# Two output projections with tokens on the partitions, norms from per-token sums, and the second layer's input transposed by diag(1/rms)

## The chip, the cores and the metric

The kernel runs on one core of one Trainium2 chip. A core has five engines with their own instruction streams: TensorE (PE, with its weight loads shown as PEld), VectorE (DVE), ScalarE (ACT), GpSimd (POOL) and SyncE (SP), which issues the transfers here. Work is held in SBUF, products are summed in PSUM, and inputs and outputs lie in DRAM. The metric is device time in microseconds (us), the median of several runs; lower is better.

## The reference

Two layers act on 256 context tokens and 256 latent tokens of width 2048. Each layer norms its input, scales and shifts it by vectors computed from a conditioning vector, projects it, mixes it in two branches, projects the result back with a 2048x2048 matrix, norms that, multiplies it by a gate vector and adds it to the stream:

```python
for i in range(DEPTH):                       # DEPTH = 2
    need_ctx = i < DEPTH - 1
    sh_x, sc_x, gt_x = jnp.split(cond_x @ ada_w[i] + ada_b[i], 3, axis=-1)
    sh_c, sc_c, gt_c = jnp.split(cond_c @ ada_w[i] + ada_b[i], 3, axis=-1)
    u_x = modulate(rms_norm(h_x, pre_g[i]), sh_x, sc_x)
    u_c = modulate(rms_norm(h_c, pre_g[i]), sh_c, sc_c)
    # i = 0: out = [conv branch | Fourier branch] @ ab_w_out
    # i = 1: out = [neighbourhood attention | S5 state space] @ cd_w_out (latents alone)
    ...
    h_x = h_x + gt_x[:, None] * rms_norm(out_x, post_g[i])
    if need_ctx:
        h_c = h_c + gt_c[:, None] * rms_norm(out_c, post_g[i])
return h_x
```

So between the layers there are two norms in a row for each token: one over the projection `out` (call its factor r1), and one over the new stream h1 = h0 + r1 * gate * post_g * out (factor r2). The second layer's input is u = h1 * r2 * A + shift, with A and the shift per feature.

## The kernel before

All arithmetic is float32. A product is built from exact halves: weights and inputs are split into a high and a low part (`split`, L70 to L76: ACT writes the high part `wh`, DVE or POOL the low part `wl`), and each product takes three matmuls (high x high, high x low, low x high). Weights stream through `load_w` (L299) as chunks of two row tiles of 512 columns, 512 KB each, loaded by SP into `raw`; eight chunks make one column group of 512 output columns over 2048 rows. `next_w` keeps three chunks ahead. `group` (its matmuls are L460) runs one column group over "blocks". A block is one accumulator, either feature-major (`mov`: a 128-column piece of the weights is stationary, the tokens move past it, and the output has features on the partitions) or token-major (`sta`: 128 tokens are stationary and the weights move past). `step` is called after each chunk: `step_ada` there does a piece of the second layer's conditioning product (`E`, L143), whose chunks SP loads as `raw<-in_ada_dram`.

The order within each engine comes from a scheduler that emits instructions by priority (`tc.high_priority()` lets a piece go earlier); only the POOL of the stretch between the layers is written out by hand (`pool_order`).

The layer-0 output projection works feature-major. Column groups n4 = 0, 1, 2 run all 512 tokens at once, with accumulators `acc`. The last one, n4 = 3, runs in two halves, hf = 0 for the context tokens and hf = 1 for the latents, with 256 columns in each matmul and accumulators `ao`. `out0_evac` empties each accumulator: ACT squares it, ACT multiplies it by the gate column (once for each half, `oG`), ACT squares that, DVE multiplies it by the residual input (`h0r`), and DVE adds the three products into running sums `aS`. `mid_chain(hf)` then turns these sums into both factors: PE sums over the partitions by a matmul with ones (`pc`, L865), DVE does two reciprocal square roots in steps on 128x2 tiles (L85 to L91) and the algebra between them, DVE writes a diagonal (`dg`, L105), PE spreads it over all partitions (`pr`, L112) and ACT copies it to SBUF (`R`, L114). With R, POOL forms h1 feature by feature (`oG*R`, L904, and `+h0s`, L905), and DVE and ACT build the input of layer 1 from it (`build_u`: DVE `w`, L183; ACT `uh`, L184; DVE `ul`, L185).

Layer 1 begins with the keys and values of the first head pair (`kv`), context tokens first and latents next, so that the first half can run while the second is normed. Then comes the S5 projection (`acc` again, token-major), and then the attention with its projections (`aq`, `ag` and others).

The layer-1 output projection is feature-major as well: 768 matmuls of 256 columns (`ao` again), ACT squares and gates each accumulator, DVE adds the squares (`sacc`). After the last matmul come the sums over partitions (`pc`), one reciprocal square root, the diagonal, its spread (`pr`), `R`, and then 32 DVE and POOL instructions on 128x256 tiles (L1419 times the factor, L1421 plus the residual) with eight output transfers of 256 KB.

Of the kernel before, what the change touches and what calls it, by code (L numbers as in the profile page):

```python
# [40 lines left out]
def tile_backbone(ctx: ExitStack, tc: tile.TileContext, a):  # L41
# [52 lines left out]
    def col_sums(psp, acc, n=4, tag="ps"):  # L94
        """acc [features, n*128 tokens] -> PSUM [tokens, n, 2] sums over the features."""
# [5 lines left out]
    def spread(psp, r, n, out, tag="ps"):  # L101
        """r [tokens, n] -> out [all partitions, n*128 tokens]."""
# [21 lines left out]
    def ada_finish(psp, l, q, es, tag="ps"):  # L124
        """es: [4 x 32 rows, 512] partial products -> columns of ada[l]."""
# [20 lines left out]
    # A = (1 + scale) * pre_g ; ada columns of chunk q < 8: [sc 2q, sc 2q+1, sh 2q, sh 2q+1]  # L146
# [14 lines left out]
    Gt = [cp.tile([P, KT, 2], F32, name="Gt%d" % l) for l in range(2)]  # L161

    def gate_cols(l):
# [15 lines left out]
    def build_u(l, kt, h, R, halves):  # L179
        """u = h * R * A + shift, split; h [P, 512] and R (per token) for the halves given."""  # L180
# [9 lines left out]
    def mm3(ps, wh, wl, xh, xl, start, stop):  # L190
        """ps += w.T @ x from the exact halves."""
# [23 lines left out]
    ss0 = cp.tile([P, 4], F32, name="ss0")  # L215
# [72 lines left out]
    wpool = ctx.enter_context(tc.tile_pool(name="wpool", reuse_waits="tile", bufs=1))  # L288
    # the chunks in the order of their use
# [22 lines left out]
    def next_w():  # L312
        """The next pair of row tiles; the loads and splits run ahead."""
# [25 lines left out]
    WAIT = 99.0  # the next part comes with the next chunk  # L339
# [23 lines left out]
    def ada_vec(l, qs, nm, pool, eng):  # L363
        """The same on VectorE or GpSimd (and ScalarE), for the first nm columns."""
# [1180 lines left out]
```

## Time and profile before

| | |
|---|---|
| median of 3 runs | 1590.17 us (1589.27 to 1592.42) |
| span of the profiled execution | 1588.4 us |
| median less span | 1.8 us |
| PE busy | 1481.1 us (93%) |
| DVE busy | 1085.7 us (68%) |
| ACT busy | 604.8 us (38%) |
| POOL busy | 306.9 us (19%) |

The profile gives the span of one execution and no time of its own beside it; the 1.8 us between the span and the median are taken as what lies around the span. In the profile's page the span is cut into 40 slices of 39.7 us. PE's busy share is nine tenths or more in nearly all of them. Exceptions are the first slice, five slices near the middle (eight, eight, nine, nine and eight tenths), which hold the stretch between the layers, and the last slice, with the end of the kernel. The granted clock of TensorE (PEclk) is full but for two slices in that same stretch and the last one. A busy PE is thus the rule, and the places where it isn't are the ones in which the order of the other engines shows.

### The profile page before, as it was taken

How to read it: one execution, taken by the hardware profiler on the slowest of the kernel's cores; microseconds unless marked ns; L12 is line 12 of the kernel's file. 1: busy time of each engine (PE TensorE's matmuls, PEld its weight loads, DVE VectorE, ACT ScalarE, POOL GpSimd, SP SyncE). 2: the span in 40 equal slices, each digit the busy share in tenths (PEclk: the TensorE clock that was granted, in tenths of full speed). 3: DMA queues.
4: the chain of work that ended last, by engine and by line, in shares of the span. 5: the costliest groups of instructions: out<-in, count | busy, mean ns of one | idle time of the engine just before them, and what ended most of it. 6: DMA issues, size and time to landing. Idle time of an engine off the chain costs nothing.

```text
span 1588.4 us, 23466 instructions
## 1 busy us (share of the span) xinstructions
PE 1481.1 (93%) x8786; PEld 1213.1 (76%) x8786; DVE 1085.7 (68%) x2460; ACT 604.8 (38%) x1155; POOL 306.9 (19%) x301
## 2 busy tenths in 40 slices
PE   3999999999999999999968899889999999999995
PEld 1556767777877657787957798777888979899995
DVE  5244999999665555674898937769597785636555
ACT  4232112121224132432533436564464554425542
POOL 0000000010020000000264605684243343000001
PEclk9999999999999999999988999999999999999997
DMA  9875444444244566653548536552232322425552
GB/s 387 346 309 211 159 159 159 159 172 166 86 159 153 185 226 210 215 191 133 176 138 280 159 117 210 168 184 101 90 124 84 110 100 98 142 83 183 187 198 80
DMA packets 80179, 269.94 MB, mean 170 GB/s; under 512 B 8513, under 2 KB 20289, under 8 KB 75329
## 3 DMA queue, kind: packets, MB, share of 16 engines
q1 hardware_dynamic: 80064, 268.44, 48.0%
q8 instruction: 69, 1.13, 0.3%
q14 instruction: 46, 0.37, 0.1%
HBM read 264.21 MB, written 4.19 MB: 169 GB/s over the span
## 4 chain that ended last, share of the span: by engine, by line
PE 69%; DVE 17%; DMA 5%; ACT 4%; issue 3%; POOL 2%; SPq 0%; DVEq 0%; ACTq 0%; POOLq 0%
PE acc L460 31%; PE kv L460 9%; PE ao L460 8%; PE E L143 4%; DVE wl L76 4%; DMA raw<-in_ada_dram 3%; PE aq L460 2%; PE ag L460 2%; PE acc L193 2%; PE acc L194 2%; PE adg L460 1%; ACT wh L73 1%; DVE w L183 1%; PE acc L192 1%; PE po L1290 1%
## 5 line engine op out<-in xcount | busy, mean ns | idle before, releaser
L73 ACT ACTIVATE wh<-raw 128x1024 fp32r<-128x1024 f32 (+1 forms) x264 | 273.3, 1039 | 574.2 <-PE acc L460 246.3
L76 DVE TENSOR_TENSOR wl<-raw,wh 128x1024 fp32r<-128x1024 f32 (+1 forms) x259 | 325.5, 1261 | 213.8 <-ACT wh L73 209.6
L495 DVE SCALAR_TENSOR_TENSOR cv<-ain,cw,cv 128x512 f32<-128x512 f32 x240 | 170.4, 749 | 0.0
L460 PE MATMUL acc<-uh,wh 128*128 128x512 f32 x400 | 160.5, 401 | 2.2 <-ACT wh L73 1.7
L460 PE MATMUL acc<-uh,wl 128*128 128x512 f32 x400 | 156.9, 397 | 2.2 <-DVE wl L76 2.2
L460 PE MATMUL acc<-ul,wh 128*128 128x512 f32 x400 | 157.4, 393 | 0.0
L460 PE MATMUL kv<-wh,uh 128*128 128x256 f32 x384 | 110.6, 288 | 3.2 <-DVE sg L1335 3.2
L460 PE MATMUL kv<-wl,uh 128*128 128x256 f32 x384 | 109.9, 286 | 0.0
L460 PE MATMUL kv<-wh,ul 128*128 128x256 f32 x384 | 109.6, 285 | 0.0
L460 PEld LDWEIGHTS acc<-uh,wh 128*128 128x128 f32 x400 | 75.4, 188 | 40.2 <-issue 10.9
L378 DVE SCALAR_TENSOR_TENSOR pa<-raw,condS,pa 128x512 f32<-128x512 f32 x90 | 63.3, 746 | 55.9 <-DMA raw<-in_ada_dram 50.1
L460 PE MATMUL kv<-ul,wh 128*128 128x512 f32 (+1 forms) x224 | 83.6, 377 | 18.2 <-DVE ul L185 18.1
L460 PEld LDWEIGHTS acc<-uh,wl 128*128 128x128 f32 x400 | 75.8, 189 | 21.1 <-DVE wl L76 2.8
L460 PE MATMUL kv<-uh,wh 128*128 128x512 f32 (+1 forms) x224 | 84.5, 391 | 3.9 <-ACT uh L184 3.9
L460 PEld LDWEIGHTS acc<-ul,wh 128*128 128x128 f32 x400 | 75.5, 189 | 16.1 <-issue 0.8
L460 PE MATMUL kv<-uh,wl 128*128 128x512 f32 (+1 forms) x224 | 82.7, 373 | 0.0
L384 POOL TENSOR_TENSOR pa<-pa,raw 128x512 f32<-128x512 f32 x45 | 64.8, 1441 | 79.1 <-ACT raw L383 77.7
L460 PEld LDWEIGHTS kv<-wh,uh 128*128 128x128 f32 x384 | 75.2, 196 | 5.8 <-DVE sg L1335 4.1
L76 POOL TENSOR_TENSOR wl<-raw,wh 128x1024 fp32r<-128x1024 f32 x5 | 12.0, 2429 | 335.5 <-DVE aS L852 333.1
L460 PEld LDWEIGHTS kv<-wl,uh 128*128 128x128 f32 x384 | 75.3, 196 | 1.8
L460 PE MATMUL acc<-wl,uh 128*128 128x512 f32 x192 | 76.5, 398 | 0.0
L460 PE MATMUL acc<-wh,ul 128*128 128x512 f32 x192 | 76.4, 398 | 0.0
(403 smaller groups left out, 3819.0 us busy)
## 6 DMA issues: line engine op xcount, KB each, us to landing
raw<-in_w_dram SPq DMA_DIRECT2D x184, 512.0 KB, 3.6
raw<-in_ada_dram SPq DMA_DIRECT2D x128, 512.0 KB, 4.8
raw<-in_wo_dram SPq DMA_DIRECT2D x72, 512.0 KB, 4.1
aw<-in_ada_dram SPq DMA_DIRECT2D x32, 1024.0 KB, 6.8
w<-in_w0a_dram SPq DMA_DIRECT2D x8, 896.0 KB, 6.8
h<-in_h_dram SPq DMA_DIRECT2D x4, 1024.0 KB, 8.3
h0r<-in_h_dram SPq DMA_DIRECT2D x16, 256.0 KB, 3.4
h0s<-in_h_dram SPq DMA_DIRECT2D x16, 256.0 KB, 4.6
```

The source lines that it names most:

```text
L73: S.activation(hi, src, AF.Copy)
L76: slo.tensor_tensor(lo, src, hi.bitcast(F32), ALU.subtract)
L143: T.matmul(E[32 * g:32 * g + 32, :], condS[:, kt, :], raw, start=(kt < 4), stop=(kt >= 12), skip_group_check=True)
L183: V.scalar_tensor_tensor(w, h[:, c], Am[l][:, kt, m:m + 1], rr, ALU.mult, ALU.mult)
L192: T.matmul(ps, wh, xh, start=start, stop=False)
L193: T.matmul(ps, wh, xl, start=False, stop=False)
L194: T.matmul(ps, wl, xh, start=False, stop=stop)
L378: V.scalar_tensor_tensor(acc, wj, c, acc, ALU.mult, ALU.add)
L384: eng.tensor_tensor(acc, acc, pr, ALU.add)
L460: T.matmul(out, lt, rt, start=st and m == 0, stop=en and m == 2, skip_group_check=True)
L495: ins = V.scalar_tensor_tensor(o, x[:, :, k:k + L], cw05[:, ch, k:k + 1], o, ALU.mult, ALU.add)
L1290: T.matmul(po, vT[:, k, i * P:(i + 1) * P], U_["PT"][:, k, :], start=k == 0, stop=k == 3)
```

## The change

Both output projections are turned token-major. An accumulator then has 128 tokens on its partitions and 512 features along the row, so a sum over features is a sum along the row: ACT's Square writes it as a by-product (`accum_out`), and no matmul with ones and no spread is needed. What was a column (the gate per feature) becomes a row that is the same on all partitions; what was a row (the factor per token) becomes a column. Layer 1 still wants features on the partitions, so h1 goes through PE once more.

- `gate_cols` becomes `gate_rows`: the gate vector is transposed on PE, copied by ACT, written to DRAM and loaded back spread over 128 partitions as 128x512 tiles (eight for layer 0, four for layer 1).
- `out0_evac` is one ACT Square with its row sum and one DVE multiply from PSUM by the gate tile. The 32 sums, 256-column evacuations and `h0r` products go.
- The last column group of layer 0 runs two blocks of 512 columns for each half: 96 matmuls of 512 columns each instead of 192 of 256.
- `mid_chain` reduces the sums, takes the root, forms h1 on DVE (8 instructions on 128x512, `oG*r1 + h0t`), squares it on ACT (8), takes the second root and writes ident * r2 for two token tiles (`dg`, 128x128 each).
- `u1_pair`: four PE matmuls on 128x128 tiles (`z`) give h1 * r2 transposed; then ACT `w<-z` with the scale A, ACT `uh`, DVE `ul`. DVE's `w` and POOL's two steps go.
- `h0t` (the residual input, token-major) is loaded once, 16 tiles of 256 KB, instead of `h0r` and `h0s`, 16 of 256 KB each.
- The conditioning product's last part for now (8 chunks, 16 `E` matmuls) falls into the last column group of layer 0 instead of the first `kv` groups.
- At the end, each token tile has its own root and four DVE instructions on 128x512 with four output transfers; the last column group runs its last three chunks block by block.

```diff
-    def out0_evac(f, ps, c):
...
-        S.activation(sq, ps, AF.Square)
-        for m, h in ((1, CT), (0, XT)):
-            if c.start <= h.start < c.stop:
-                o = h.start - c.start
-                S.activation(oG[f][:, h], ps[:, o:o + L], AF.Copy, scale=Gt[0][:, f, m:m + 1])
-        S.activation(s3, oG[f][:, c], AF.Square)
-        pr = h0r[f][:, c]
-        V.tensor_tensor(pr, oG[f][:, c], pr, ALU.mult)
-        for acc, t in zip(aS, (sq, pr, s3)):
...
+    def out0_evac(t, n4, ps):
...
+        jk = scr.tile([P, 512], F32, tag="t512", name="jk")
+        S.activation(jk, ps, AF.Square, accum_out=ssq[:, 0, t, n4:n4 + 1])
+        V.tensor_tensor(oG[t][n4], ps, gts[n4, 1 - t // 2], ALU.mult)
...
     def mid_chain(hf):
...
+            r1 = token_rsqrt(ssq[:, 0, ts, :], 2, "r1_%d" % hf, "r2")
+            for i in range(2):
+                t = 2 * hf + i
+                for c in range(4):
+                    o = oG[t][c]
+                    V.scalar_tensor_tensor(o, o, r1[:, i:i + 1], h0t[t, c], ALU.mult, ALU.add)
+                    jk = scr.tile([P, 512], F32, tag="t512", name="jk")
+                    S.activation(jk, o, AF.Square, accum_out=ssq[:, 1, t, c:c + 1])
+            r2 = token_rsqrt(ssq[:, 1, ts, :], 2, "r2_%d" % hf, "r2")
+            dg = l0.tile([P, 2, P], F32, tag="pa%d" % hf, name="dg")
+            for i in range(2):
+                V.tensor_scalar(dg[:, i, :], ident, r2[:, i:i + 1], None, ALU.mult)
...
+    def u1_pair(hf, p, pool, tag):
...
+                T.matmul(z[:, j, i * P:(i + 1) * P],
+                         oG[2 * hf + i][kt // 4][:, (kt % 4) * P:(kt % 4 + 1) * P],
+                         dgs[hf][:, i, :], start=True, stop=True)
...
+            S.activation(w, z[:, j, :], AF.Copy, scale=Am[1][:, kt, m:m + 1])
+            S.activation(uh[kt][:, c], w, AF.Identity, bias=sh_col(1, kt, m))
+            V.scalar_tensor_tensor(ul[kt][:, c], w, sh_col(1, kt, m), uh[kt][:, c].bitcast(F32),
+                                   ALU.add, ALU.subtract)
...
+    for hf in range(2):
+        group(KORD0, [blk(accs[t], 0, 512, sta=lambda k, t=t: mtok(k, t))
+                      for t in (2 * hf, 2 * hf + 1)], tail=2, step=step_pairs)
+        for t in (2 * hf, 2 * hf + 1):
+            out0_evac(t, 3, accs[t])
+        mid_chain(hf)
```

DVE at the end of the first half's chain, before. `rr` holds the factors, `dg` is the diagonal that PE's spread waits for, and `w` is the first step of layer 1's input.

```order
L89 TENSOR_TENSOR r2t<-rr 128x2
L90 TENSOR_TENSOR r2t<-r2t,r2n 128x2
L91 SCALAR_TENSOR_TENSOR rr<-r2t,rr 128x2
L105 TENSOR_TENSOR dg<-ident,rr 128x512
L76 TENSOR_TENSOR wl<-raw,wh 128x1024 x2
L183 SCALAR_TENSOR_TENSOR w<-oG_4933,Am_81,R_0_6137 128x256
L852 TENSOR_TENSOR aS_4376<-aS_4376,ev 128x256
```

DVE at the same place after: the context tokens' second chain (`r_0`, ending in `dg`), with the last accumulator of the latents (`ao_5551`), the latents' sums and a weight split between its steps.

```order
L91 SCALAR_TENSOR_TENSOR r_0_5786<-r2t,r_0_5786 128x2
L853 TENSOR_REDUCE sm<-ssq 128x2
L848 TENSOR_TENSOR oG_5540<-ao_5551,gt 128x512
L89 TENSOR_TENSOR r2t<-r_0_5786 128x2
L855 TENSOR_SCALAR ms<-sm 128x2
L90 TENSOR_TENSOR r2t<-r2t,r2n 128x2
L76 TENSOR_TENSOR wl<-raw,wh 128x1024
L87 TENSOR_SCALAR r2n<-ms 128x2
L91 SCALAR_TENSOR_TENSOR r_0_5786<-r2t,r_0_5786 128x2
L85 TENSOR_SCALAR r2t<-ms 128x2
L875 TENSOR_SCALAR dg<-ident,r_0_5786 128x128 x2
```

The context tokens' diagonal stands behind the multiply of the last accumulator, where before it stood some 20 instructions ahead of the latents' evacuation.

ACT at the beginning of layer 1, before: the latents' last evacuation (`ev`, `oG`) stands among the first pieces of layer 1's input (`uh`).

```order
L840 ACTIVATE ev<-ao_5632 128x256
L844 ACTIVATE oG_5875<-ao_5632,Gt_82 128x256
L184 ACTIVATE uh_6215<-w,ada_79 128x256
L845 ACTIVATE ev<-oG_5875 128x256 x2
L73 ACTIVATE wh<-raw 128x1024
L184 ACTIVATE uh_6221<-w,ada_79 128x256
```

ACT at the same place after: `ao_5550` and `ao_5551` are the latents' accumulators, and `w<-z` is the first step of layer 1's input, of the context tokens.

```order
L847 ACTIVATE jk,ssq<-ao_5550 128x512
L847 ACTIVATE jk,ssq<-ao_5551 128x512
L73 ACTIVATE wh<-raw 128x1024
L871 ACTIVATE jk,ssq<-oG_4940 128x512 x2
L871 ACTIVATE jk,ssq<-oG_5536 128x512 x2
L871 ACTIVATE jk,ssq<-oG_4944 128x512 x2
L871 ACTIVATE jk,ssq<-oG_5540 128x512 x2
L893 ACTIVATE w<-z,Am_81 128x256 x4
L894 ACTIVATE uh_6047<-w,ada_79 128x256
```

The eight squares of the latents' h1 (L871) now stand ahead of the first piece of the context tokens' input.

DVE at the end of the kernel, before: the root's last step, the diagonal, and the pairs on 128x256 tiles that follow.

```order
L91 SCALAR_TENSOR_TENSOR r2y<-r2t,r2y 128x2
L105 TENSOR_TENSOR dg<-ident,r2y 128x256
L1419 TENSOR_TENSOR oF_13951<-oF_13951,pr 128x256
L1419 TENSOR_TENSOR oF_13956<-oF_13956,pr 128x256
L1421 TENSOR_TENSOR hxkT<-hxkT,oF_13951 128x256
L1421 TENSOR_TENSOR hxkT<-hxkT,oF_13956 128x256
```

DVE at the end after: `ao_13857` is the last accumulator, `rf` the factors of a token tile (two of them, one after the other), `hx` the residual and result.

```order
L87 TENSOR_SCALAR rfn<-ms 128x1
L1388 TENSOR_TENSOR o1VT<-ao_13857,g_3_13392 128x512
L853 TENSOR_REDUCE sm<-ssf 128x1
L86 TENSOR_SCALAR rf_13997<-rft 128x1
L855 TENSOR_SCALAR ms<-sm 128x1
L89 TENSOR_TENSOR rft<-rf_13997 128x1
L90 TENSOR_TENSOR rft<-rft,rfn 128x1
```

The first tile's root, whose sums are ready earlier, stands behind the multiply that waits for the last matmul, so nearly all of both roots follows that matmul.

## Rows read from the trace of the kernel before

**Rows 1.** By stretch: start:end, length, busy PE, PEld, DVE, ACT, POOL; clock, DMA, GB/s.

```profile
680.00:725.00 45.00, 45.00 (x199) 36.90 (x197) 33.27 (x46) 16.71 (x25) 0.00 (x0) 1.00 0.54 180
...
760.00:800.00 40.00, 39.46 (x334) 39.26 (x333) 32.54 (x52) 20.52 (x32) 12.02 (x5) 1.00 0.56 191
800.00:840.00 40.00, 26.00 (x154) 22.72 (x155) 37.00 (x60) 16.12 (x31) 27.72 (x31) 0.79 0.46 157
840.00:880.00 40.00, 33.07 (x216) 26.57 (x214) 32.52 (x66) 15.28 (x21) 21.00 (x24) 0.91 0.72 239
880.00:920.00 40.00, 34.91 (x194) 34.33 (x195) 33.90 (x86) 18.63 (x43) 19.02 (x25) 0.91 0.51 158
1478.00:1570.00 92.00, 90.96 (x771) 90.54 (x769) 45.14 (x55) 43.39 (x68) 0.00 (x0) 1.00 0.48 162
```

**Rows 2.** Chain that ended last, 660 to 1590: start, us, what.

```profile
668.45 66.09 PE acc L460 x288
...
758.32 29.20 PE ao L460 x246
...
947.75 1.89 PE aq L460 x14
...
1477.84 90.53 PE ao L460 x768
```

**Rows 3.** DVE one by one, first half's chain: start, us, what.

```profile
795.03 2.33 DVE L89 TENSOR_TENSOR r2t<-rr 128x2 f32<-128x2 f32 x1
797.39 0.16 DVE L90 TENSOR_TENSOR r2t<-r2t,r2n 128x2 f32<-128x2 f32 x1
...
802.32 0.69 DVE L105 TENSOR_TENSOR dg<-ident,rr 128x512 f32<-128x512 f32 x1
```

**Rows 4.** POOL at the same time.

```profile
787.86 9.49 POOL L76 TENSOR_TENSOR wl<-raw,wh 128x1024 fp32r<-128x1024 f32 x4 [2.35 <-ACT wh L73]
```

**Rows 5.** PE behind that chain, idle time in brackets.

```profile
803.16 1.72 PE L112 MATMUL pr<-dg,ones 128*128 128x512 f32 x2 [3.69 <-DVE dg L105]
...
820.31 0.58 PE L460 MATMUL kv<-ul,wh 128*128 128x256 f32 x1 [4.67 <-DVE ul L185]
```

**Rows 6.** Costliest groups by form, 758.3 to 947.7: count, busy, mean ns, idle before.

```profile
L76 DVE TENSOR_TENSOR wl<-raw,wh 128x1024 fp32r<-128x1024 f32 x35 | 47.4, 1359 | 30.8 <-ACT wh L73 30.7
L73 ACT ACTIVATE wh<-raw 128x1024 fp32r<-128x1024 f32 x40 | 42.2, 1059 | 51.5 <-PE ao L460 15.7 <-PE acc L460 12.5 <-DMA raw<-in_w_dram 8.8
...
L904 POOL TENSOR_TENSOR oG<-oG,R 128x256 f32<-128x256 f32 x32 | 33.0, 1033 | 26.3 <-ACT R L114 26.3
...
L183 DVE SCALAR_TENSOR_TENSOR w<-oG,Am,R 128x256 f32<-128x256 f32 x32 | 25.4, 800 | 1.9 <-POOL oG L905 1.9
...
L185 DVE SCALAR_TENSOR_TENSOR ul<-w,ada,uh 128x256 fp32r<-128x256 f32 x32 | 23.3, 742 | 1.2 <-ACT uh L184 1.2
...
L143 PE MATMUL E<-raw,condS 128*32 128x512 f32 x32 | 7.4, 605 | 0.0
...
L844 ACT ACTIVATE oG<-ao,Gt 128x256 f32<-128x256 f32 x8 | 3.8, 473 | 0.0
...
L852 DVE TENSOR_TENSOR aS<-aS,s 128x512 f32<-128x512 f32 x3 | 2.0, 683 | 0.0
...
L840 ACT ACTIVATE sq<-acc 128x512 f32<-128x512 f32 x2 | 1.2, 591 | 0.0
```

**Rows 7.** PE's waits in the same stretch: total, times, longest.

```profile
PE kv L460 <- DVE ul L185: 18.1, 8, 4.7
```

**Rows 8.** The chain around float32 matmuls of 127 and 129 columns.

```profile
405.57 0.45 PE Y L570 x4
```

**Rows 9.** The end, all engines, one by one.

```profile
1568.08 0.28 PE L460 MATMUL ao<-nh,wl 128*128 128x256 f32 x1
...
1584.53 0.74 DVE L1421 TENSOR_TENSOR hxyT<-hxyT,oF 128x256 f32<-128x256 f32 x2
```

**Rows 10.** Transfers issued at the end: KB each, us to landing.

```profile
out_dram<-hxyT SPq DMA_DIRECT2D x2, 256.0 KB, 2.0
```

More of the change, by code (lines that the diff above doesn't have):

```diff
@@ L907, in u1_pair, with h0_load @@
-    def u1_pair(hf, p):
-        c = (CT, XT)[hf]
-        for kt in (2 * p, 2 * p + 1):
+    h1d = dps.tile([2, P, D], F32, name="h1d")
+    mtok = lambda k, t: (mh[k][:, t * P:(t + 1) * P], ml[k][:, t * P:(t + 1) * P])
+    oG = [[None] * 4 for _ in range(4)]
+    ssq = l0.tile([P, 2, 4, 4], F32, tag="s5_sums", name="ssq")
+    h0t, gts = {}, {}
+    def h0_load(t, c):
+        i = (4 * t + c) % 8
+        h = (l0.tile([P, 512], F32, tag="X%d" % i, name="h0t") if i < 4
+             else l0a.tile([P, 512], F32, tag="ain", name="h0t", bufs=5))
+        nc.sync.dma_start(h, a["h0t"][t][:, 512 * c:512 * c + 512])
+        h0t[t, c] = h
@@ L915, in tile_backbone @@
     for n4 in range(3):
         out0_open(n4)
[L917 to L919 removed]
+        if n4 == 2:
+            for t, c in ((t, c) for t in range(2) for c in range(4)):
+                h0_load(t, c)
+        o = group0(KORD0, sta=mtok)
+        for t in range(4):
+            out0_evac(t, n4, o[t])
     pump(1e9)
@@ L968, in kv_blocks @@
         return bl
+    pairs = iter([(0, p, psA, "acc") for p in range(4, 8)])
     kv_acc = [psp.tile([P, 512], F32, tag="ps", name="kv%d" % i) for i in range(4)]
-    group(kts, kv_blocks([0]), step=step_chain)
-    for _ in chain:
-        pass
-    u1_half(1, range(8))
-    group(kts, kv_blocks([1]), step=step_ada)
+    group(kts, kv_blocks([0]), step=step_pairs)
+    for p in range(4):
+        u1_pair(1, p, psA, "acc")
+    pairs = iter([(1, p, psA, "acc") for p in range(4, 8)])
+    group(kts, kv_blocks([1]), step=step_pairs)
     epool[:] = [psp, "ps"]
-    for kt in range(KT):
-        nc.sync.dma_start(h1d[kt], oG[kt][:, XT])
-    pool_order.close()
+    for t in range(2):
+        for c in range(4):
+            nc.sync.dma_start(h1d[t][:, 512 * c:512 * c + 512], oG[2 + t][c])
     lay0.close()
@@ L1408, in tile_backbone @@
[L1408 to L1424 removed]
+    ntok = lambda k, t: (nh[k][:, t * P:(t + 1) * P], nl[k][:, t * P:(t + 1) * P])
@@ new lines, in tile_backbone @@
+    hxt = [l1.tile([P, 2, 512], F32, tag=tg, name="hx" + tg) for tg in ("kT", "vT", "PT", "yT")]
+    hx = [[hxt[2 * t + c // 2][:, c % 2, :] for c in range(4)] for t in range(2)]
+    for i in range(4):
+        nc.sync.dma_start(hxt[i].rearrange("p c f -> p (c f)"),
+                          h1d[i // 2][:, 1024 * (i % 2):1024 * (i % 2) + 1024])
+    g1 = []
+    for c, tg in enumerate(("uh14", "ul14", "uh15", "ul15")):
+        g1.append(up.tile([P, 512], F32, tag=tg, name="g1_%d" % c))
+        gate_tile(1, 0, c, g1[c])
@@ new lines, in tile_backbone @@
+    o0 = l1.tile([P, 4, 512], F32, tag="U", name="o0")
+    oF = [[o0[:, c, :] for c in range(4)],
+          [l1.tile([P, 512], F32, tag=tg, name="o1" + tg) for tg in ("bias", "qT", "sg", "VT")]]
+    ssf = l1.tile([P, 2, 4], F32, tag="ssf", name="ssf")
+    for n4 in range(4):
+        accs = [acc_tile("ao%d" % t) for t in range(2)]
+        group(KORD1, [blk(accs[t], 0, 512, sta=lambda k, t=t: ntok(k, t)) for t in range(2)],
+              tail=3 if n4 == 3 else 1)
+        for t in range(2):
+            jk = scr.tile([P, 512], F32, tag="t512", name="jk")
+            S.activation(jk, accs[t], AF.Square, accum_out=ssf[:, t, n4:n4 + 1])
+            V.tensor_tensor(oF[t][n4], accs[t], g1[n4], ALU.mult)
+            if n4 == 3:
+                r = token_rsqrt(ssf[:, t:t + 1, :], 1, "rf%d" % t, "rf")
+                for c in range(4):
+                    V.scalar_tensor_tensor(hx[t][c], oF[t][c], r, hx[t][c], ALU.mult, ALU.add)
+                    nc.sync.dma_start(a["out"][t][:, 512 * c:512 * c + 512], hx[t][c])
```

209 lines of the change are left out of this document (57 added, 152 removed).

## The prediction

> **What bounds the kernel now.** I read the busy time by stretch first, to find where PE isn't the bound; then the chain that ended last, for the borders of the stages; then the groups by form and the waits inside the stretch that isn't full. The reader is to see three things.
>
> First, in the layer-0 output projection's first three column groups PE is busy all the time: 45.00 of 45 us [rows 1]. The chain passes there through 288 matmuls of 512 columns in 66.09 us [rows 2], 0.2295 us each. The layer-1 output projection is full as well, 90.96 of 92 us [rows 1], as 768 matmuls of 256 columns in 90.53 us [rows 2], 0.1179 each. In both, an evacuation is hidden behind matmuls, and making it cheaper pays nothing.
>
> Second, from the last column group's beginning at 758.3 to the first `aq` at 947.75 [rows 2] lie 189.4 us. The products in it, on an unhindered PE, are 384 `ao` at 0.1187 (29.20 us for 246 [rows 2]) = 45.6; 384 `kv` of the same width at 0.1179 = 45.3; 192 `acc` at 0.2295 = 44.1; `E` 7.4 [rows 6] and its transposes, some 0.7. That is 143.1, so 46.3 us go elsewhere. Between 760 and 920 PE is idle for 26.6 us (160 less the four busy times), and by the mean clocks 0.79, 0.91 and 0.91 it stands 31.2 us at 1.2 instead of 2.4 GHz, which costs up to 15.6 [rows 1]. The waits are for DVE: `ul` holds `kv` for 18.1 us in eight waits [rows 7], the diagonal holds the spread for 3.69 [rows 5]. DVE is late because it shares with POOL: one of the chain's 128x2 steps took 2.33 us beside POOL's weight splits and 0.16 behind them [rows 3, 4]; `w` takes 800 ns and `ul` 742 on 128x256 [rows 6], while a plain 128x512 with two SBUF inputs takes 683 there [rows 6].
>
> Third, the end: from the last matmul (1568.36) to the span's end (1588.4) are 20.0 us, of which 3.1 follow the last DVE instruction (1585.27) [rows 9], with a transfer that takes 2.0 to land [rows 10].
>
> **The stretch after, part by part.** Products: 192 `ao` of 512 columns at 0.2295 = 44.1 (1.5 less than before), `kv` 45.3, `acc` 44.1, `E` with transposes 8.1. Added are 64 `z` matmuls in float32 on 128 columns. The nearest row has 0.45 us for four records of such matmuls, two records each [rows 8]: 0.225 each, 14.4 in all. From below, the 0.118 of a 256-column product would make it 7.6; from above, the same rows at half clock 28.8. I take the row, since its form is nearly the same. The sums and spreads (`pc`, `pr`) go with their waits. Work: 156.0.
>
> Stalls come in two places. (a) In the second half of the last column group, DVE has to do the context chain ahead of the split of chunk 7: some 2 us until the first half's last square and multiply, 13 small steps at 0.19 (26 of them from 797.39 to 802.32 [rows 3]) = 2.5, up to four POOL splits of 2.4 that block them [rows 4], 8 instructions on 128x512 at 0.683 = 5.5, and the split, 1.36: 20.9 us into the half. PE has done its first six chunks and the `E` work by then, at about 18. I take 3 us (0 if POOL's splits lie elsewhere, 8 if those eight instructions stretch beside POOL as `w` does).
>
> (b) At the end of that group, time T0. DVE's queue has the square's reduction and the last multiply ahead of the context diagonal: 0.9 until ACT's square is done (591 ns [rows 6] after 0.3 of waiting), 0.2, 0.7, six small steps 1.2, a weight split 1.4, the diagonals 0.2: `z` starts at T0 + 4.6. All 32 context `z` run in a row, 7.2, to T0 + 11.8. But ACT's first `w<-z` stands behind the eight squares of the latents, whose inputs DVE makes behind that chain: ten small steps (6.6), 8 at 0.683 (12.1), the last square 12.7. Four `w` at 0.473 and one `uh` at about 0.5 [rows 6]: `kv` starts at T0 + 15.1. So 4.6 + 3.3 = 7.9 us of idle PE. Queued behind ACT's squares are the `uh` of the context tokens alone, and only `kv` waits for these.
>
> After that `kv` isn't starved: ACT needs 0.47 + 0.5 for each row tile and half a weight split of 1.06 [rows 6], 1.5, against 12 matmuls = 1.41, and it is ahead by the time `kv` begins the latents, whose diagonal is long done. POOL's 32 `oG*R` of 1033 ns [rows 6] and as many additions are gone, so DVE isn't slowed.
>
> Half clock: before, 26.6 us of idle brought up to 15.6 of loss. For 10.9 of idle, in the same proportion, 6 us (0 to 15.6).
>
> Sum: 156.0 + 10.9 + 6 = 172.9, against 189.4: **16.5 gained**.
>
> The Trainium skill's page "TensorE: Matmul & The Clock Gate", Part 4: PE-mode transpose, says that a transpose does not count as PE activity in the way a matmul does. Here `z` is an ordinary matmul with a diagonal, and no row of before shows 32 in a row; if they counted as nothing, the idle time at T0 would be one of 15.1 us and `z` itself would run at half clock, 7.2 us dearer in each half. That is inside the range below.
>
> **The other parts.** Gate rows and `h0t`: their transfers are issued long before use; the DMA share is about one half there [rows 1] and 4 MB fewer are loaded than before, against 3 MB of gate tiles; nothing. `h1d` writes stand behind nothing urgent; nothing. Layer-1 output: 384 matmuls of 512 at 0.2295 = 88.1 against 90.5: **2.4 gained** (0 if 512 columns bring no better price there).
>
> The end: from the last matmul, 0.3, the multiply 0.68, the reduction 0.2, 12 small steps 2.3 (mostly the first tile's root, which waited behind that multiply), four on 128x512 2.7, 11 small steps 2.1, four more 2.7: 11.0, and 3.1 as before: 14.1 against 20.0, **5.9 gained**. It would be 8 if the first root fell before the last matmul, and 4.5 if each step on 128x512 took 0.8.
>
> In all 24.8: the profiled execution goes from 1588.4 to 1563.6, and the median of the runs, 1.8 above it, from 1590.17 to **1565.4**.
>
> **Rivals.**
> 1. The chains hide: `z` starts at T0 and ACT finds time, so that no stall and no half clock is left. For it: DVE has little else to do. Against: the order of DVE and ACT at T0. Work 156.0 alone: 33.4 + 8.3 = 41.7 gained, **1548.5**.
> 2. `kv` stays starved in part, by ACT, which now has `w` and `uh` for each row tile where it had `uh` alone. For it: 1.5 against 1.41. Stalls and half clock 29 instead of 17: **1577.5**.
> 3. The stretch doesn't do what it says: the waits only change their names, 42.2 us of idle and half clock (26.6 + 15.6) stay beside 156.0. That is 198.2, 8.8 more, against 8.3 gained elsewhere: **1590.7**, no change. For it: eight waits of before, at the same handing-over of weights and inputs. Against: POOL is out of it.
> 4. Slower: the clock stays low. If TensorE falls to 1.2 GHz in the idle time at T0, as it did behind the 3.69 us wait [rows 5, 1], and the `z` pieces and short waits keep it there to the end of `kv`, then 59.7 us of work (14.4 + 45.3) double: 53.7 beyond the 6 already counted, **1619.1**. It decides from some 25 us of such work beyond that 6. Against: before, the clock came back within a few us each time, 31.2 us at half in 160 with eight waits and more.
>
> **How the numbers follow.** The forecast's own range, 1554 to 1577, holds 0.60: the bounds of (a), of `z` and of half clock shift it by about 11 either way. Rival 1 has 0.12, rival 2 (1577 to 1587) 0.14, rival 3 (within 0.2%, about 3 us, what a measurement of this kernel can tell from no change) 0.06, rival 4 0.08. For 8 in 10, I leave out half of rival 1, rivals 3 and 4 and a little: 1550 to 1586. Faster is the first three, 0.86; same 0.06; slower 0.08.
>
> **What would show it.** In the profile after: PE busy above nine tenths in the first half of the last column group; one wait of 2 to 5 us of `z` for `dg`, one of 3 us of `kv` for ACT, and hardly any of `kv` for `ul`; 170 to 176 us from the first `ao` to the first `aq`; `z` at 0.225 us; 88 us for the last projection; 14 us from the last matmul to the end. Wrong would be: many waits of `kv` for ACT, a clock under 0.8 for the whole of `kv`, or a new wait elsewhere (the first three column groups waiting for a gate tile, chunks late behind the `h0t` loads).

## The result, and the profile after

The changed kernel takes 1564.96 us (median of 4 runs, 1562.3 to 1567.83) beside 1590.91 us of the kernel before (4 runs on the same chip, 1589.27 to 1592.42). The ratio is 0.9835, with a 95% interval of 0.9816 to 0.9853. The forecast was 1565.4. The profiled execution was the quickest of the four, with a span of 1560.5 us against 1588.4.

The sum is right to half a microsecond. That is partly luck, as a cut of the two spans at the same marks shows. S is the begin of layer 0's last column group, where the stretch begins: its first `E` after, its first `ao` before. The mark near 650 is the end of the conditioning transposes `ept`. The gain is in us:

| part of the span | before | after | gain | forecast |
|---|---|---|---|---|
| start to the mark near 650 | 650.4 | 642.6 | 7.8 | 0 |
| from there to S (rest of the first three column groups) | 107.8 | 108.9 | -1.1 | 0 |
| S to the first `aq` (the stretch) | 189.6 | 170.6 | 19.0 | 16.5 |
| first `aq` to the last projection | 529.9 | 536.1 | -6.2 | 0 |
| last projection | 90.7 | 87.3 | 3.4 | 2.4 |
| last matmul to the span's end | 20.1 | 15.1 | 5.0 | 5.9 |
| span | 1588.4 | 1560.5 | 27.9 | 24.8 |

The three parts with a forecast gained 27.4 where 24.8 was forecast. The first part and the fourth, forecast at nothing, run all but the same instructions in both kernels and moved by 7.8 and -6.2. (120 of the projection's first 576 matmuls lie ahead of the mark; up to the first of them the gain is 7.0 already, 618.7 against 611.7.) So the rows after are read in three questions: what is left of the stalls in the stretch, what stands at the end, and why unchanged code runs at another pace.

First the stretch by windows: start:end, length, busy PE, PEld, DVE, ACT, POOL; then clock, DMA share, GB/s. They answer to [rows 1].

```profile
751.50:786.00 34.50, 34.50 (x144) 21.35 (x144) 10.63 (x10) 11.17 (x13) 1.21 (x1) 1.00 0.68 229
786.00:814.00 28.00, 22.32 (x92) 17.39 (x93) 25.14 (x57) 15.38 (x32) 10.70 (x5) 0.93 0.72 238
814.00:825.00 11.00, 9.95 (x72) 9.56 (x72) 9.60 (x31) 9.09 (x27) 1.75 (x5) 0.86 0.63 234
825.00:850.00 25.00, 25.00 (x213) 25.00 (x212) 15.47 (x24) 18.32 (x36) 0.00 (x0) 1.00 0.44 148
```

From 825 on PE is full at the full clock; the granted clock fell in 786 to 825 only. The waits of PE from 640 to 935 (waited for: total, times, longest) are all that is left of [rows 7]:

```profile
PE z L885 <- DVE dg L875: 3.9, 1, 3.9
PE ao L469 <- POOL wl L76: 1.7, 1, 1.7
PE acc L469 <- DVE oG L848: 1.6, 1, 1.6
PE kv L469 <- ACT uh L894: 1.0, 1, 1.0
```

Eight waits of `kv` for `ul`, 18.1 us, have become none. The third row lies ahead of the stretch and was not forecast. The groups by form in 751.4 to 922 (count, busy, mean ns, idle before) show what stands behind that:

```profile
L894 ACT ACTIVATE uh<-w,ada 128x256 fp32r<-128x256 f32 x32 | 14.9, 532 | 0.0
L895 DVE SCALAR_TENSOR_TENSOR ul<-w,ada,uh 128x256 fp32r<-128x256 f32 x32 | 14.6, 492 | 2.6 <-ACT uh L894 2.5
...
L869 DVE SCALAR_TENSOR_TENSOR oG<-oG,r,h0t 128x512 f32<-128x512 f32 x16 | 12.9, 879 | 0.1
```

`ul` takes 492 ns instead of 742 [rows 6], at the same shape, now that POOL is empty beside it, and DVE's `w` (25.4 us [rows 6]) is gone.

The context chain, by DVE's and then POOL's timeline (start, us, what):

```profile
788.48 1.09 DVE L855 TENSOR_SCALAR ms<-sm 128x2 f32<-128x2 f32 x1
...
789.69 2.38 DVE L87 TENSOR_SCALAR r2n<-ms 128x2 f32<-128x2 f32 x1
...
792.17 0.16 DVE L89 TENSOR_TENSOR r2t<-r 128x2 f32<-128x2 f32 x1
...
792.57 2.27 DVE L91 SCALAR_TENSOR_TENSOR r<-r2t,r 128x2 f32<-128x2 f32 x1
...
796.05 7.51 DVE L869 SCALAR_TENSOR_TENSOR oG<-oG,r,h0t 128x512 f32<-128x512 f32 x8
...
815.12 5.39 DVE L869 SCALAR_TENSOR_TENSOR oG<-oG,r,h0t 128x512 f32<-128x512 f32 x8
```

```profile
784.79 7.26 POOL L76 TENSOR_TENSOR wl<-raw,wh 128x1024 fp32r<-128x1024 f32 x3 [340.12 <-ACT wh L73]
792.43 2.40 POOL L76 TENSOR_TENSOR wl<-raw,wh 128x1024 fp32r<-128x1024 f32 x1 [0.38 <-ACT wh L73]
799.98 2.36 POOL L76 TENSOR_TENSOR wl<-raw,wh 128x1024 fp32r<-128x1024 f32 x1 [5.15 <-ACT wh L73]
```

The reader is to compare ends. POOL's three splits in a row end at about 787.2, 789.6 and 792.05, the fourth at 794.83. `ms` ends at 789.57, `r2n` at 792.07, `r` at 794.84: each of these 128x2 steps is held until a split ends, while `r2t` in POOL's gap takes 0.16. The eight `oG` steps carry the fifth split in the same way: 7.51 us here, 5.39 for the same eight at 815.12, with POOL idle.

### The profile page after: what moved, and what is told of

It is laid out like the page before. It is cut to its first block, busy times and chain, and to the rows that moved or that the text cites. A ratio compares the mean times of both kernels' runs of the same rounds, so it can differ in the third digit from the quotient of the medians.

```text
span 1560.5 us, 22281 instructions
## 1 busy us (share of the span) xinstructions
PE 1476.7 (95%) x8306; PEld 1192.1 (76%) x8306; DVE 1026.0 (66%) x2364; ACT 599.0 (38%) x1162; POOL 241.2 (15%) x229
## 4 chain that ended last, share of the span: by engine, by line
PE 71%; DVE 16%; DMA 6%; ACT 3%; issue 2%; POOL 2%; SPq 0%; DVEq 0%; ACTq 0%; POOLq 0%
PE acc L469 31%; PE kv L469 11%; PE ao L469 7%; DMA raw<-in_ada_dram 5%; PE E L143 5%; DVE wl L76 3%; PE acc L204 2%; PE aq L469 2%; PE ag L469 2%; PE acc L205 2%; PE adg L469 1%; PE acc L203 1%; PE po L1271 1%; POOL pa L393 1%; ACT wh L73 1%
## 5 line engine op out<-in xcount | busy, mean ns | idle before, releaser
L393 POOL TENSOR_TENSOR pa<-pa,raw 128x512 f32<-128x512 f32 x45 | 65.9, 1467 | 87.3 <-ACT raw L392 84.8
L469 PE MATMUL acc<-wh,mh 128*128 128x512 f32 x192 | 75.4, 395 | 1.6 <-DVE oG L848 1.6
L469 PE MATMUL acc<-wh,uh 128*128 128x512 f32 x192 | 76.1, 398 | 0.0
```

What stands on the lines that cost most here:

```text
L393: eng.tensor_tensor(acc, acc, pr, ALU.add)
L469: T.matmul(out, lt, rt, start=st and m == 0, stop=en and m == 2, skip_group_check=True)
```

## The experiments

Every run was timed against the kernel before on its own chip; the ratio's 95% interval is in brackets. "Stretch" is S to the first `aq`, in us of the profiled execution.

"512 columns" and "256 columns" are the mean time between the starts of consecutive matmuls of that width, from 150 to 650 us and in the 400 us behind the first `aq`.

| run | median us | ratio | stretch | projection | end | 512 columns, ns | 256 columns, ns |
|---|---|---|---|---|---|---|---|
| before, again (one run) | 1593.41 | | 189.1 | 90.7 | 20.1 | 230.26 | 116.00 |
| after, again | 1568.21 | 0.9843 [0.9827, 0.9859] | 170.7 | 87.3 | 15.2 | 227.71 | 119.04 |
| tail pinned | 1565.74 | 0.9833 [0.9816, 0.9849] | 171.0 | 87.3 | 12.5 | 227.75 | 119.06 |
| 256 columns in layer 1 | 1567.03 | 0.9838 [0.9823, 0.9853] | 170.6 | 91.8 | 13.9 | 227.76 | 119.06 |
| shift | 1570.45 | 0.9858 [0.9823, 0.9892] | 170.5 | 87.7 | 15.0 | 227.83 | 119.09 |
| shift weights | 1573.0 | 0.9891 [0.9859, 0.9923] | 170.3 | 89.8 | 15.0 | 233.01 | 117.16 |
| shift inputs | 1576.15 | 0.9904 [0.9878, 0.993] | 169.9 | 89.7 | 15.1 | 233.07 | 117.15 |
| POOL busy | 1575.99 | 0.9903 [0.9875, 0.9931] | 180.5 | 87.3 | 14.9 | 227.72 | 119.09 |
| distance 192 | 1568.84 | 0.9854 [0.9831, 0.9877] | 169.4 | 89.6 | 15.1 | 230.21 | 115.84 |
| tail pinned, distance 0 | 1563.7 | 0.9823 [0.9802, 0.9845] | 170.6 | 87.3 | 12.5 | 227.75 | 119.06 |
| tail pinned, distance 128 | 1572.73 | 0.9875 [0.9856, 0.9894] | 170.9 | 89.4 | 12.4 | 232.25 | 118.36 |
| splits on DVE | 1564.32 | 0.9822 [0.9797, 0.9846] | 167.2 | 87.3 | 14.8 | 227.70 | 119.05 |

**Both kernels again.** No edit.

> The changed kernel once more, unchanged, for a second trace. In the first pair of traces the changed kernel is 7.9 us ahead when the conditioning transposes at 650 us begin, in code that is the same in both, and loses 6.2 us between the first aq and the last projection, in code that is also the same there; a matmul of 256 columns takes 115.6 to 116.4 ns there before and 118.8 to 119.0 after. Theory W (the spacing of matmuls wanders from one execution to the next): this trace need not repeat either, each may differ by several us in either direction. Theory G (a denser TensorE stream is paid back later by wider spacing): 118.5 to 119.5 ns again, and 534 to 538 us from the first aq to the last projection. Theory L (the start is really faster, by another layout of the inputs): the transposes at 642 us again, to within 1 us. The stretch from the last column group to the first aq should repeat in all theories: 169 to 172 us, and the end 15 us.

> The kernel before once more, unchanged, for a second trace. Theory W: the common start and the part from the first aq to the last projection differ from the first trace (650.4 and 529.9 us) by some us, and from e1 by less than the first pair does. Theory G: 115.6 to 116.5 ns for 256 columns between 950 and 1350 us, 529 to 531 us for that part. Theory L: the transposes at 650 us again. The stretch from the last column group to the first aq: 189 us in all, the end 20 us.

The stretch, the projection and the end repeat within 0.5 us in either kernel. The two unchanged parts don't: the 650 mark came at 647.8 in this trace of after and 649.9 in that of before, and first `aq` to last projection took 534.8 and 534.0, where the first traces have 536.1 and 529.9. So of the 7.8 and -6.2 in the table above a good part is one execution against another; a steady part had to be looked for in the pace of the matmuls.

**The tail pinned.** The last projection's final chunks are written token tile by token tile, but in the trace PE alternates between the tiles' accumulators. The edit chains those matmuls in the written order.

```diff
-                        T.matmul(out, lt, rt, start=st and m == 0, stop=en and m == 2,
+                        mm = T.matmul(out, lt, rt, start=st and m == 0, stop=en and m == 2,
...
+                        if len(kps) > 1:
+                            hold(mm)
...
-              tail=3 if n4 == 3 else 1)
+              tail=3 if n4 == 3 else 1, hold=pin if n4 == 3 else (lambda x: x))
```

> One edit to the changed kernel: the last three chunks of the last column group are held in program order, so that the first token tile's 18 matmuls end 4.1 us ahead of the second tile's. In the changed kernel they alternate in fives and the first tile's root waits behind the last multiply. If the roots behind the last matmul are what makes the end 15.1 us where 14.1 was forecast: the first tile's root (2.5 us) and its squares fall beside matmuls, 13 us from the last matmul to the end, 2 gained. Rival: the end is set by the output transfers (2.5 to 2.8 us to landing now, 2.0 before) and not by the roots: 15 us as now.

The end took 12.5 instead of 15.1 us. DVE's timeline of this run; its last matmul starts at 1550.09:

```profile
1550.26 1.41 DVE L1394 SCALAR_TENSOR_TENSOR hxkT<-o,rf,hxkT 128x512 f32<-128x512 f32 x2
...
1552.91 0.68 DVE L1390 TENSOR_TENSOR o1VT<-ao,g 128x512 f32<-128x512 f32 x1
...
1558.00 0.75 DVE L1394 SCALAR_TENSOR_TENSOR hxyT<-o1VT,rf,hxyT 128x512 f32<-128x512 f32 x1
```

The first tile's root is now done by the last matmul, as the prediction's "8 if the first root fell before the last matmul" has it; DVE then does that tile's four steps ahead of the second tile's multiply, which waits for them until 1552.91. The gain at the end, 7.6 in all, is in the trace; in the medians 2.6 us are within the intervals.

**256 columns in layer 1.** The last projection's matmuls as before, two of 256 columns for each of 512; all else as after.

```diff
-        group(KORD1, [blk(accs[t], 0, 512, sta=lambda k, t=t: ntok(k, t)) for t in range(2)],
+        group(KORD1, [blk(accs[t][:, c:c + L], c, c + L, sta=(lambda k, t=t: ntok(k, t)), first=c == 0)
+                      for t in range(2) for c in (0, L)],
```

> One edit to the changed kernel: the layer-1 output projection in blocks of 256 columns, 768 matmuls again, all else as changed. If the wider matmul is what takes the projection from 90.7 to 87.3 us: 90 to 91 us again from the first to the last ao, 3 slower. Rival: it was the pace of that execution or the lighter evacuation: no more than 88.

The projection took 91.8 against 87.3: in this layout the wider matmul is what shortened it. Some of that came back at the end (13.9 against 15.1), and the medians can't be told apart.

**Three shifts of the layout.** In the trace of after, matmuls of 512 columns in layer 0's first part follow each other in 227.7 ns, of before in 230.2; those of 256 columns in layer 1 in 119.1 against 116.0. Their instructions are the same; what differs is where their operands lie in SBUF. The edits move a 32x128 gate tile into scratch and add padding ahead of the layer's inputs, ahead of the weights, or both; no instruction's work changes.

```diff
# all three
-        gr = sp.tile([32, P], F32, tag="gr", name="gr")[0:16 * n]
+        gr = scr.tile([P, 512], F32, tag="t512", name="gr")[0:16 * n, 0:P]
# shift, shift inputs
+    cp.tile([P, 8], F32, name="cpad")
# shift weights, shift inputs
+    sp.tile([P, 8], F32, name="spad")
```

> The changed kernel with 32 bytes more on each partition ahead of the layer inputs (uh, ul, mh, ml) and of the weights (raw, wh, wl), so that both begin 32 bytes off a multiple of 64 again, as in the kernel before; in the changed kernel both lie on multiples of 64. Every engine's instructions and their order stay the same (only the small gate tile gr moves to a scratch tile). So far the spacing of matmuls went with the kernel and not with the execution: 512 columns from 150 to 650 us 230.1 and 230.3 ns in two traces of before, 227.7 to 227.8 in four of the changed kernel; 256 columns behind the first aq 116.0 twice, 119.0 to 119.1 four times. Theory A (addresses): 230 and 116 ns, the conditioning transposes at 649 to 650 us, 530 to 534 us from the first aq to the last projection. Theory G (denser work is paid back later): 227.7 and 119 as in the changed kernel, 535 to 538 us.

> The same with only the weights (and scratch tiles) 32 bytes off, the layer inputs on multiples of 64. Theory A: the two spacings go with one of the two operands each, or with the two standing alike. If a matmul of 256 columns is quicker when the stationary and the moving operand stand differently, 116 here as well as in the other mixed kernel; if it needs the layer inputs off the multiple, 119 here. For 512 columns (layer inputs stationary in some, moving in others) 227.7 if the layer inputs decide, 230 if the weights do. Theory G: 227.7 and 119.

> The same with only the layer inputs 32 bytes off and the weights on multiples of 64. Theory A: the opposite of the other mixed kernel where one operand decides; if one of the two mixed kernels has both the quick 512 (227.7) and the quick 256 (116), it is about 5 us quicker than the changed kernel, 1562 us. Theory G: 227.7 and 119, no difference.

The theory that an operand's own alignment sets the pace fell: "shift" kept both spacings of after (227.83 and 119.09), and the other two gave 233.0 and 117.15, a third pair, the one wide spacing slower, the other quicker. What sorts the pairs is the distance in SBUF between the first weight tile and the first tile of layer inputs, by the addresses that the compiled programs give them: 90816 bytes in before, 91392 in after, 90880 in "shift", 90912 in the other two. To the modulus of 256 these are 192, 0, 0, 32 and 32.

**Distance 192.** The changed kernel with the distance brought to 91328, which is 192 as in before.

```diff
+    sp.tile([P, 112], F32, name="spad")
-        gr = sp.tile([32, P], F32, tag="gr", name="gr")[0:16 * n]
+        gr = scr.tile([P, 512], F32, tag="t512", name="gr")[0:16 * n, 0:P]
```

> The changed kernel with the weights moved by 448 bytes less than nothing else: instructions and order as in the changed kernel, layer inputs on the same addresses. The shifts so far rule out that a multiple of 64 matters by itself, but sort by one number, the distance from the first layer input (uh0) to the first weight tile (wh), modulo 512 bytes: 192 in the kernel before (230.2 ns for 512 columns from 150 to 650 us, 116.0 ns for 256 behind the first aq), 256 in the changed kernel and in e5 (227.8, 119.1), 288 in both mixed shifts (233.0, 117.2, twice the same to 0.1). Theory D (this distance sets the spacing): with 192 here, 230.1 to 230.3 and 115.9 to 116.1 ns, as before the change, the conditioning transposes near 650 us and 530 to 534 us from the first aq to the last projection. Rival: something else that came with the change (the longer dense stretch between the layers, other tiles) sets them, and 227.8 and 119.1 stay.

The same stretch of the chain (start, us, what) of before, after, distance 192 and shift inputs, 48 matmuls each, with the change to `E` behind them:

```profile
231.97 11.19 PE acc L460 x48
```

```profile
228.11 11.11 PE acc L469 x48
```

```profile
232.09 11.20 PE acc L470 x48
```

```profile
233.20 11.40 PE acc L471 x48
```

With the distance of before, the changed kernel has the spacings of before: 230.21 and 115.84 ns. So the pace of unchanged code came from the layout, not from the new work. In this layout the change does 1593.25 to 1568.84 on one chip, 24.4 us gained, and the parts of its profiled execution say the same: stretch 20.2, projection 1.1, end 5.0, and -1.9 from the 650 mark to S, together 24.4.

**Distances 0 and 128**, both with the tail pinned.

```diff
+    sp.tile([P, 64], F32, name="spad")      # distance 0; 96 for distance 128
-        gr = sp.tile([32, P], F32, tag="gr", name="gr")[0:16 * n]
+        gr = scr.tile([P, 512], F32, tag="t512", name="gr")[0:16 * n, 0:P]
```

> The changed kernel with its last chunks held in order (as e3, 2.6 us quicker at the end) and the distance between layer inputs and weights at 0 modulo 512. Theory D: spacings of its own, the same for the whole run, not those of the changed kernel; which, no run says yet: between 226 and 233 ns and between 115 and 120. If 512 columns stay at 227.8 or less and 256 come near 116, it beats the changed kernel by 5 us beyond the 2.6. Rival: 227.8 and 119.1, and 2.6 us quicker alone, 1565.5.

> The same with the distance at 128 modulo 512. Theory D: spacings of its own again, between 226 and 233 ns and between 115 and 120; it beats e10 if its sum over some 2700 matmuls of 512 columns and 3900 of 256 is smaller. Rival: 227.8 and 119.1, 1565.5.

At 91136 the spacings are those of after at 91392, to 0.05 ns: 256 bytes further on nothing differs, as far as these two and "shift" show. At 91264, 128, they are 232.25 and 118.36, and the run is 9 us slower than distance 0; their intervals don't meet. Distance 0 gave 1563.7, the lowest median of all runs, though its interval overlaps that of after.

**POOL busy.** 64 POOL multiplies of 128x256 beside `kv`, whose result nothing uses: the work that the change took from POOL, put back without its dependences.

```diff
+    pb = [l0.tile([P, 512], F32, tag="X%d" % i, name="pb%d" % i) for i in range(2)]
...
+    for i in range(64):
+        G.tensor_tensor(pb[0][:, 0:L], pb[0][:, 0:L], pb[1][:, 0:L], ALU.mult)
```

> The changed kernel with 64 additional multiplies on 128x256 on POOL, on two tiles that nothing else uses any more, begun when the latents' residual is done and run beside kv: as many as the kernel before had there. They add nothing to the result. Theory P (POOL beside DVE is what made ul and w late and starved kv before): ul goes from 0.44 to about 0.74 us and the weight splits with it, DVE needs 1.4 us for each row tile where TensorE needs 1.41, and kv waits for ul again: 3 to 12 us more from the last column group to the first aq. Rival: before, kv waited because DVE had one instruction more (w) for each row tile, and the chain stood in its way; POOL beside it costs under 2 us.

The stretch grew by 9.9 us. Groups by form in it, and then waits of PE:

```profile
L955 POOL TENSOR_TENSOR pb<-pb,pb 128x256 f32<-128x256 f32 x64 | 63.8, 997 | 5.0
L76 DVE TENSOR_TENSOR wl<-raw,wh 128x1024 fp32r<-128x1024 f32 x35 | 50.0, 1440 | 34.2 <-ACT wh L73 34.1
...
L895 DVE SCALAR_TENSOR_TENSOR ul<-w,ada,uh 128x256 fp32r<-128x256 f32 x32 | 26.8, 880 | 0.3
```

```profile
PE acc L469 <- DVE wl L76: 2.6, 1, 2.6
PE kv L469 <- DVE ul L895: 1.9, 1, 1.9
```

Nothing uses POOL's results, and yet `ul` goes from 492 to 880 ns: sharing with POOL alone slows DVE. DVE's busy time in the stretch is 144.8 us before, 124.2 here and 98.9 after, so sharing makes some 25 of the 46 us that the change took from it.

The waits come back to a much smaller part. Of the 9.9 us, 5.6 are idle time of PE and some 5 are clock (mean 0.95 in the stretch against 0.98). `kv` waits for `ul` once, 1.9 us, where it waited 18.1 before. The other wait shown, 2.6 us, seems to come from how the edit was made. The load of `bcT` was issued as POOL's multiplies end (887.61), in after at 864.95, and DVE stood for it with the split that `acc` needs behind it; `bcT` lies in a pool that is opened when that of the scratch tiles `pb` is closed, so it probably had to wait for their memory. SP's and DVE's timelines:

```profile
887.64 0.33 SPq L1034 DMA_DIRECT2D bcT<-in_sb_dram  x1
```

```profile
889.73 0.24 DVE L658 TENSOR_TENSOR tq<-bcT,coef 128x64 f32<-128x64 f32 x1 [6.80 <-DMA bcT<-in_sb_dram]
...
892.29 1.63 DVE L76 TENSOR_TENSOR wl<-raw,wh 128x1024 fp32r<-128x1024 f32 x1
```

So POOL's share in the old stalls is shown for the pace of DVE's steps, and for little of the 18.1 us of waits. The multiplies ran in one piece from 818.9 to 887.6 us, the old ones in two from 805.6 to 890, so the run may understate it. The change also took `w` (25.4 us [rows 6]) out of DVE and made the chains shorter; which of these ended the rest of the waits was not tried apart.

The Trainium skill, page "SBUF — State Buffer", section "Who interferes with whom", says that a DVE instruction with two SBUF inputs, or in a two-port mode, and a GpSimd instruction that reads SBUF shut each other out for a whole instruction. The ends in the two fences of the context chain agree, and so do 880 ns of `ul` beside POOL's 997 ns.

**Splits on DVE.** The five weight splits that POOL does for the last column group are given to DVE.

```diff
-... + ((G,) if nm == "wo0" and n == 4 and kp in range(2, 7) else ())
+... + ((V,) if nm == "wo0" and n == 4 and kp in range(2, 7) else ())
```

> One edit to the changed kernel: the five weight splits that POOL does in the latents' half of the last column group are done by DVE. In the changed kernel three 128x2 steps of the context chain take 1.1, 2.4 and 2.3 us beside them, TensorE waits 1.7 us for a POOL split and 3.9 us for the diagonal. If POOL's blocking is what makes the diagonal late: those three steps take 0.2, but DVE has five splits of 1.24 = 6.2 us more in its queue, so that the two nearly cancel: the wait for POOL goes, the wait for the diagonal is 3 to 5 us, the stretch 169 to 172 us. If DVE had time to spare in that half, the diagonal is ready at its end and the stretch is 165 us. Rival on the other side: the splits stand ahead of the chain, and the chunks behind it are late, 175 us.

The stretch fell by 3.4, to 167.2. Waits of PE, and DVE's timeline in the chain:

```profile
PE z L885 <- DVE dg L875: 3.7, 1, 3.7
...
PE ao L469 <- DVE wl L76: 0.6, 1, 0.6
```

```profile
794.48 0.16 DVE L87 TENSOR_SCALAR r2n<-ms 128x2 f32<-128x2 f32 x1
...
797.07 0.16 DVE L91 SCALAR_TENSOR_TENSOR r<-r2t,r 128x2 f32<-128x2 f32 x1
...
800.06 5.39 DVE L869 SCALAR_TENSOR_TENSOR oG<-oG,r,h0t 128x512 f32<-128x512 f32 x8
```

No step of 128x2 is held any more, the eight `oG` take 5.39, and the wait in the middle of the group falls from 1.7 to 0.6, though DVE now does five more splits of 1.22 us. Of the 3.4 us, 1.3 are idle time (waits of 5.3 against 6.6) and some 1.7 clock (mean 0.99 in the stretch against 0.98). The wait of `z` for the diagonal stays at 3.7: there the small steps alternate with splits and multiplies in DVE's own queue. The median, 1564.32, can't be told from that of after. This edit and the pinned tail at distance 0 were not run together.

## Why the prediction was right, step by step

**What bounds the kernel.** Right in that the stalls of the stretch were waits for DVE, and that DVE's steps are slowed by sharing with POOL (`ul` 492 or 880 ns). That sharing is why `kv` starved is shown in small part only: with POOL busy again, 1.9 of the 18.1 us of waits for `ul` came back. The page of before has its gaps in two places, not in the stretch alone: six, eight and eight tenths of PE from 794 to 913, and eight and eight tenths from 993 to 1072, behind the first `aq`, which the change leaves as it is.

**The `z` matmuls.** 0.225 us each was taken from [rows 8], between 0.118 and twice 0.225. In the second half, at the full clock, the chain has

```profile
847.25 4.91 PE z L885 x44
```

two records to a matmul: 0.223. The half-clock bound for them fell too: the 32 in a row behind the longest wait took 9.0 us, where half clock all through would make 14.3, and the clock was 1.00 from 825 on. The rule on transposes that the prediction weighed, of the Trainium skill's page "TensorE: Matmul & The Clock Gate", Part 4: PE-mode transpose, does not show for these matmuls by a diagonal. The granted clock was 0.57 at their begin, behind the longest wait, and back at 1.00 for the rest, while `z` alone ran on PE (windows as above):

```profile
813.20:817.10 3.90, 3.90 (x20) 3.90 (x21) 3.55 (x14) 1.19 (x3) 0.00 (x0) 0.57 0.49 175
817.20:822.20 5.00, 5.00 (x45) 4.82 (x44) 4.05 (x12) 5.00 (x17) 0.10 (x1) 1.00 1.04 374
```

The prediction's range has a slip here: its upper bound for `z`, 28.8, is 14.4 above its sum, and alone would give 1579.8. That lies outside 1554 to 1577, and "about 11 either way" does not cover it; only the range for 8 in 10, 1550 to 1586, does.

**The stalls.** PE by its timeline, at the three waits of the stretch:

```profile
802.39 0.50 PE L469 MATMUL ao<-wl,mh 128*128 128x512 f32 x1 [1.70 <-POOL wl L76]
...
813.20 9.01 PE L885 MATMUL z<-dg,oG 128*128 128x128 f32 x64 [3.88 <-DVE dg L875]
...
823.24 0.50 PE L469 MATMUL kv<-uh,wh 128*128 128x256 f32 x2 [1.02 <-ACT uh L894]
```

All three came where they were forecast: 3 us in the group's middle (1.7), `z` at T0 + 4.6 (T0 + 3.9), and `kv` at T0 + 15.1 (T0 + 13.9). At the distance of before, the last two are 4.6 and 14.7. Idle in all is 6.6 against 10.9.

**Half clock.** Forecast 6 us. By the windows, (1 - 0.93) x 28 + (1 - 0.86) x 11 = 3.5 us of clock were not granted.

**The sum of the stretch.** 172.9 was forecast, 170.6 measured: 4.3 less idle and 2.5 less half clock, but some 4.5 more work than 156.0. The chain of the stretch (start, us, what) shows most of it:

```profile
752.53 5.67 PE ao L469 x24
...
865.45 11.51 PE kv L469 x96
876.97 39.61 PE acc L469 x168
```

`ao`, with the changes to and from `E` between its pieces, takes 0.2362 for each matmul and `acc` 0.2358, where both were priced at 0.2295: 192 x 0.0067 and 192 x 0.0063, 2.5 us. `kv` takes 0.1199 instead of 0.1179: 0.8. The other 1.2 are not assigned to an instruction. So two errors cancelled in part. Before, the same stretch holds 27 us of idle time and, by its mean clock of 0.92, some 15 of clock not granted: the change took away 20 and 12 of these and paid for them with 13 us more work.

**DVE's 128x512 steps.** The price of 683 ns [rows 6] was right where POOL rests (5.39 for eight, 0.67) and low where it works (7.51, 0.94); the mean, 879, mixes both.

**The last projection.** Forecast 2.4, measured 3.4, of which the layout gave 2.3: at the distance of before it is 1.1 (89.6 against 90.7, 0.2333 for each matmul). Neither layout gives the 2.4; that it lies between the two is luck. The prediction priced 512 columns at 0.2295; the row of after is

```profile
1458.31 86.04 PE ao L469 x379
```

0.2270 each.

**The end.** Forecast 14.1, measured 15.1. The timeline from the last matmul on, to be held against [rows 9], and the last transfers (KB each, us to landing):

```profile
1545.08 0.39 PE L469 MATMUL ao<-wh,nl 128*128 128x512 f32 x1
1545.09 0.69 DVE L1388 TENSOR_TENSOR o<-ao,g 128x512 f32<-128x512 f32 x1 [5.43 <-ACT jk L1387]
...
1546.22 0.69 DVE L1388 TENSOR_TENSOR o1VT<-ao,g 128x512 f32<-128x512 f32 x1
...
1555.58 0.75 DVE L1392 SCALAR_TENSOR_TENSOR hxyT<-o1VT,rf,hxyT 128x512 f32<-128x512 f32 x1
```

```profile
out_dram<-hxyT SPq DMA_DIRECT2D x2, 256.0 KB, 2.8
```

The last DVE step ends 10.9 us behind the last matmul's end (1556.33 less 1545.47), where 11.0 was forecast. What was mis-sized is the term behind it: 3.1 was carried over, and it took 4.2, with transfers that land in 2.8 us instead of 2.0 [rows 10]. Eight of 256 KB now leave within 7 us, where before they took 9; that their crowding is the reason was not tried. The prediction's 4.5 for steps of 0.8 us should be 5.0 by its own terms (eight steps, 0.117 dearer each).

**What was costed at nothing and wasn't.** The prediction said that cheaper evacuations pay nothing in the first three column groups, and that is so; but a new wait came, which it did not name. DVE's and PE's timelines:

```profile
701.37 2.74 DVE L387 SCALAR_TENSOR_TENSOR pa<-raw,condS,pa 128x512 f32<-128x512 f32 x4 [3.91 <-DMA raw<-in_ada_dram]
704.03 1.22 DVE L76 TENSOR_TENSOR wl<-raw,wh 128x1024 fp32r<-128x1024 f32 x1
705.16 1.88 DVE L848 TENSOR_TENSOR oG<-acc,gt 128x512 f32<-128x512 f32 x3
```

```profile
705.90 0.50 PE L469 MATMUL acc<-wh,mh 128*128 128x512 f32 x1 [1.59 <-DVE oG L848]
```

Before, ACT alone emptied these accumulators; now DVE's multiply does so too, and in DVE's queue it stands behind conditioning steps that wait 3.91 us for a chunk to land, and behind a split. PE stands for 1.6 us, and the 650 mark to S grew by 1.1. But the wait is not steady: in the second trace of after it is 0.3 us, and that part takes 107.7, as before the change (107.8). At distance 192 it is 0.2, and that part grew by 1.9 for another reason: its 512-column matmuls, in which the weights now move and the tokens stand still, follow each other in 232.1 ns against 228.9 before, 1.5 us for the 455 in it.

**The rivals.** Rival 1 (no stall left) is excluded by the 3.9 us wait; rival 2 by a single wait of 1.0 us of `kv` for ACT; rival 3 by a stretch of 170.6 where it had 198.2; rival 4 by the clock of 1.00 from 825 on.

## What to carry to other kernels

When an engine is late, look at what runs beside it as well as at its own work: here moving work off POOL made a step of DVE that stayed a third shorter, and with POOL busy again most of the waits still stayed away. When the engine that empties an accumulator changes, read the new engine's queue for what may stand ahead of it, DMA waits above all. And before a few microseconds of unchanged code are put down to the change, run the kernel with a padding that restores the old layout.

## What was not expected of the hardware

The spacing of matmuls at the full clock depends on where their operands lie: 227.7 to 233.1 ns for 512 columns and 115.8 to 119.1 for 256, steady to 0.2 ns for each layout, the same 256 bytes further on, and best for the two widths at different distances. It depends on which operand moves as well: with the tokens moving 228.9 ns in the first output projection before, with the weights moving 232.1 at the same distance. Beyond the sorting by distance nothing on its cause was tried; it stays open. In time, after and distance 192 differ by less than their intervals (0.9843 [0.9827, 0.9859] and 0.9854 [0.9831, 0.9877]), while distances 0 and 128 differ by more.
